# SwiGLU in three 256-column matmuls, and TensorE's tiles on a 256 B grid with the weights 64 B and 192 B off it

## The chip, the cores and the metric

The kernel runs on one core of a Trainium2 chip, in float32 throughout. The metric is the time of one execution on the device, in microseconds (us). The kernel before takes 1268.25 us in the median of three runs (1267.49 to 1269.01).

## What is computed

Two layers over a sequence of 256 positions of width 1024. Per layer: a SwiGLU block, a mixer, a second SwiGLU block. Cut to what matters here:

```python
for l in range(DEPTH):                                   # 2
    x = x + 0.5 * swiglu(rms_norm(x, ffn1_norm[l]), ffn1_w_gate[l], ffn1_w_up[l], ffn1_w_down[l])
    h = rms_norm(x, mix_norm[l])
    proj = h @ w_in[l] + b_in[l]                         # 1024 -> 7176: q k v f xr gr gA gR
    ...                                                  # attention with forget gates; conv + RG-LRU scan
    merged = sigmoid(g_attn) * y_attn + sigmoid(g_rnn) * y_rnn
    x = x + merged @ w_out[l]
    x = x + 0.5 * swiglu(rms_norm(x, ffn2_norm[l]), ffn2_w_gate[l], ffn2_w_up[l], ffn2_w_down[l])
# swiglu(x, g, u, d) = (silu(x @ g) * (x @ u)) @ d, 1024 -> 2816 -> 1024
```

## The kernel before

**Products.** Activations lie transposed (128 channels by 256 positions). For float32 accuracy on TensorE's fast `float32r` format every operand is split into a high part and a low rest: `split` (line 270) copies the high part on ScalarE and subtracts on VectorE. A product of one 128x128 weight block with one 128x256 block of activations is hi*hi + hi*lo + lo*hi, accumulated in a PSUM bank. It comes in two forms (`product`, line 252):

- `mm3` (line 246): three matmuls of 256 columns. The stationary operand is the high weight block in the first two and the low one in the third; each matmul loads its stationary block anew. The mixer's column products take this form: per layer 32 blocks of 8 for xr, gr, gA and gR (256 products), 24 blocks of 8 for the two branch outputs and the merge (192), and 16 in the recurrence (`recurrence`), 464 in all.
- `sides`: one matmul of 512 columns with the high weights, over the high and the low activations side by side (the low half falls into the bank's second half), and one of 256 columns with the low weights. `total` (line 261) then adds the two halves: a copy on ScalarE into the tile `tot` and an addition on VectorE. SwiGLU takes this form (`SIDES = True`): 22 x 2 x 8 products for gate and up and 176 for the way down, 528 a block, 2112 in the four blocks, with 52 calls of `total` a block.

The q, k, v projections (`rows` in `mix`) turn the roles round: activations are stationary and 512 columns of weights stream, 192 threes of 512-column matmuls in both layers.

**Weights.** They arrive in pieces of 1 MB (`wr<-ws` in the trace, three tiles `wr`), are split half a piece at a time (`split_half`, line 364) and wait as a pair of 128x1024 tiles, high and low, either in the eight tiles `W` or in free ones of the 21 tiles `R`. The moving activations are the tile `xs` (the normed input) or tiles `R` (hidden values, branch outputs) or `S`. A planner walks over the steps in order while the program is built; it gives each engine's queue its order, by modelled costs, and splits weights ahead where ScalarE and VectorE have room.

**Where tiles lie.** SBUF tiles are placed one after another in order of first use, each rounded up to 32 B, after a 16 KiB area for DMA descriptors. `R` is 1036 floats wide, so neighbouring ones start 4160 B apart, which is 64 B more than a multiple of 256. In the program that this kernel builds the starts, modulo 256, are: `xs` and all `W` 128; `R0`, `R1`, `R2`, `R3`, `R4`, ... 0, 64, 128, 192, 0, ...; `S` 0, 0, 0, 128, 128. The trace leaves buffer numbers out. In the built program the stretches quoted below use these (starts modulo 256):

| stretch, us | moving | high weights | low weights |
|---|---|---|---|
| 371.8 to 383.8 | xs 128 | W 128 | W 128 |
| 309.5 to 312.0 | xs 128 | R1 64 | R3 192 |
| 406.6 to 408.0 | R17, R1 64 | W3 128 | W2 128 |
| 417.8 to 419.2 | R17, R1 64 | W1 128 | W0 128 |
| 486.1 to 497.4 and 511.3 to 522.4 | xs 128 | W 128 | W 128 |

Blocks inside a tile are a multiple of 512 B apart, so each block of a tile has its tile's start modulo 256.

Of the kernel before, what the change touches and what calls it, by code (L numbers as in the profile page):

```python
# [23 lines left out]
F32 = mybir.dt.float32  # L24
F32R = mybir.dt.float32r
# [23 lines left out]
AHEAD = 20  # L49
SLACK = 2.0  # L50
EARLYX = -0.4
SIDES = True


def f32(ap):
# [138 lines left out]
class Trunk:  # L194
    def __init__(self, ctx, tc, ws, xT, prm, wf, wbd, b_in, out):
        self.tc = tc
        self.ws, self.xT_in, self.prm, self.wf, self.wbd, self.b_in, self.out = ws, xT, prm, wf, wbd, b_in, out
        pool = lambda name, **k: ctx.enter_context(tc.tile_pool(name=name, **k))
        self.const = pool("const", bufs=1)
        self.sb = pool("sb", bufs=1)  # L200
        self.ps = pool("ps", bufs=1, space=bass.MemoryType.PSUM)
        self.dram = pool("dram", bufs=1, space=bass.MemoryType.DRAM)
        ctx.enter_context(tc.manual_schedule())
        nc = tc.nc
        self.clock = c = Clock()
        self.made = {}
        self.PE, self.ACT, self.DVE, self.POOL, self.SP = (Queue(c, nm, e) for nm, e in (
            ("PE", nc.tensor), ("ACT", nc.scalar), ("DVE", nc.vector), ("POOL", nc.gpsimd), ("SP", nc.sync)))
        self.big = Places(c, lambda i, dt: self.t([128, 1036], f"R{i}", 1, dt), 21)
        self.halves = Places(c, lambda i, dt: self.t([128, 1024], f"W{i}", 1, dt), 8)  # L210
        self.small = Places(c, lambda i, dt: self.t([128, 512], f"S{i}", 1, dt), 5)
        self.banks = Places(c, lambda i, dt: self.ps.tile([128, 512], F32, tag=f"B{i}", name=f"B{i}", bufs=1), 8)
        self.steps, self.tasks, self.starts = [], [], []
        self.n_halves = self.s = 0
        self.hl, self.r, self.rb, self.raw, self.acc, self.xs_ok = {}, {}, {}, {}, {}, set()
        self.phase = 0


    def t(self, shape, tag, bufs, dt=F32):
        tl = self.sb.tile(shape, dt, tag=tag, name=tag, bufs=bufs)  # L220
        old = self.made.setdefault(tag, [])
        if len(old) >= bufs:
            self.clock.touch[tl.tensor.name] = self.clock.touch.get(old[-bufs], 0.0)
        old.append(tl.tensor.name)
        return tl
# [3 lines left out]
            self.push()  # L229
        return places.take(dt)  # L230

    def slot(self, shape, dt=F32):

        tl = self.take(self.big, dt)
        return tl, self.view(tl, shape)

    @staticmethod
    def view(tl, shape):
        v = tl[:, :math.prod(shape)]
        if len(shape) == 1:  # L240
            return v
        names = "abcd"[:len(shape)]
        return v.rearrange(f"p ({' '.join(names)}) -> p {' '.join(names)}", **dict(zip(names, shape)))
# [108 lines left out]

    def load_piece(self, p, w=slice(0, 2048)):
        if p not in self.raw:
            self.raw[p] = self.t([128, 2048], "wr", 3)
        self.SP.dma_start(out=self.raw[p][:, w], in_=self.ws[p, :, w])

    def split_places(self):
# [2 lines left out]
            return self.halves  # L361
        return self.big if len(self.big.idle) >= SPARE else None

    def split_half(self, j):
        while self.loaded < self.n_halves // 2 and self.loaded <= j // 2 + 2:
            self.load_piece(self.loaded)
            self.loaded += 1
        places = self.split_places()
        hi, lo = (places.take(F32R)[:, :1024] for _ in range(2))
        raw = self.raw[j // 2][:, (j % 2) * 1024:(j % 2 + 1) * 1024]  # L370
        self.split(hi, lo, raw)
        self.hl[j] = hi, lo, places
        if j % 2:
            del self.raw[j // 2]

    def first_halves(self):

        for j in range(2):
            self.hl[j] = *(self.halves.take(F32R)[:, :1024] for _ in range(2)), self.halves
        for i, (j, c) in enumerate(((0, 0), (1, 0), (0, 1), (1, 1))):  # L380
            for k in (2 * i, 2 * i + 1):
                self.scale_x(0, "ffn1", k)
            w = slice(c * 512, c * 512 + 512)
            self.split(self.hl[j][0][:, w], self.hl[j][1][:, w], self.raw[0][:, j * 1024 + c * 512:j * 1024 + c * 512 + 512])
        del self.raw[0]
# [62 lines left out]
    def new_x(self, phase, l, norm, k):  # L448

        yield self.when(self.x)  # L450
        if k == 0:
            self.xs = self.t([128, 8, 512], "xs", 1, F32R)
        self.scale_x(l, norm, k)
        self.xs_ok.add((phase, k))
        yield self.when(after=0.5)
        self.squares(phase, k)
        if k == 7:
            self.spawn(self.stats(phase), "stats")
# [40 lines left out]
    def setup(self):  # L499
        c = self.const  # L500
        self.cpad = c.tile([128, 128], F32, name="cpad")
        self.DVE.memset(self.cpad, 0.0)
        self.fpad = c.tile([128, 256], F32, name="fpad")
        self.POOL.memset(self.fpad, 0.0)
        self.prm_sb = c.tile([128, L, NP_], F32, name="prm")
        self.ACT.dma_start(out=self.prm_sb, in_=self.prm)
        self.ACT.activation(self.t([128, 1], "ss", 4), self.cpad[:, 0:1], AF.Silu)
        self.x = c.tile([128, 8, 256], F32, name="x")
        q = lambda i: slice(512 * i, 512 * i + 512)
        for i, w in enumerate((0, 2, 1, 3)):  # L510
            self.SP.dma_start(out=self.x[:, 2 * i:2 * i + 2], in_=self.xT_in[:, 2 * i:2 * i + 2])
            self.load_piece(0, q(w))
        self.load_piece(1, slice(0, 1024))
        self.load_piece(1, slice(1024, 2048))
        self.load_piece(2)
        warm = self.take(self.banks)
        for _ in range(WARM):
            self.PE.matmul(warm[:, 0:128], self.cpad, self.cpad, start=True, stop=True)
        self.banks.give(warm)
        self.ident = c.tile([128, 128], F32, name="ident")  # L520
        self.POOL.memset(self.ident, 1.0)
        self.POOL.affine_select(out=self.ident, in_=self.ident, compare_op=ALU.is_equal, fill=0.0, base=0,
                                pattern=[[-1, 128]], channel_multiplier=1)
        self.ones = c.tile([128, 128], F32, name="ones")
        self.POOL.memset(self.ones, 1.0)
        self.mhalf = c.tile([128, 8], F32, name="mhalf")
        self.DVE.memset(self.mhalf, -0.5)
        self.xs = self.t([128, 8, 512], "xs", 1, F32R)
        self.xs_ok |= {(0, k) for k in range(8)}
        self.spawn(self.first_stats(), "stats")  # L530
        self.starts.append((30, self.constants, "bias"))
# [59 lines left out]
    def ffn(self, l, name):  # L591
# [3 lines left out]

        def gu_steps(f):
            js = self.half(), self.half()
            banks = {}

            def step(i, ks):  # L600
                def fn(wh, wl):
                    if ks[0] == 0:

                        self.need(lambda: phase in self.rb or len(self.banks.idle) > 1, "stats", "x")
                        banks[i] = self.take(self.banks)
                    for k in ks:
                        w = slice(k * 128, k * 128 + 128)
                        self.product(banks[i], wh[:, w], wl[:, w], self.x_rhs(phase, k), k == 0, k == 7, SIDES)
                return Step(js[i], fn, [(self.glu(f, phase, banks, st), "glu")] if i and ks[-1] == 7 else [])
            if f == 0 and not self.steps:  # L610
                order = [(i, ks) for ks in (range(4), range(4, 8)) for i in range(2)]
            elif f == 0:
                order = [(0, range(4)), (0, range(4, 7)), (1, range(4)), (1, range(4, 7)), (0, range(7, 8)), (1, range(7, 8))]
            else:
                order = [(i, ks) for i in range(2) for ks in (range(4), range(4, 8))]
            self.steps += [step(i, ks) for i, ks in order]

        for f in range(NF):
            gu_steps(f)
        halves = [self.half() for _ in range(NF)]  # L620
        runs = {}
        for i in range(8 * NF):
            d, f = divmod(i, NF)
# [49 lines left out]
    def mix(self, l):  # L673
# [6 lines left out]
        def rows(i):  # L680

            nm, n = PROJ[i]
            js = [self.half() for _ in range(4)]
            banks = {}

            def step(h, t):
# [88 lines left out]
    def block_diagonal(self, M):  # L775
        for n in range(2):
# [1 line left out]
            raw, w = self.slot([4, 2, 128])  # L778
            self.SP.dma_start(out=w, in_=self.wbd[M["l"], n])
            yield self.when(raw, must=lambda: len(self.big.idle) >= 4)  # L780
            hi, lo = (self.slot([4, 2, 128], F32R) for _ in range(2))
            self.split(hi[1], lo[1], w)
            self.big.give(raw)
            M["wd", n] = hi, lo
# [419 lines left out]
```

## Time and profile before

| | us |
|---|---|
| median of three runs | 1268.25 |
| the profiled execution: its own time | 1267.97 |
| its span, first to last instruction | 1266.3 |
| TensorE busy, matmuls | 1255.5 |
| VectorE busy | 937.3 |
| ScalarE busy | 755.0 |

What lies around the span is 1.67 us; the median run is 0.28 us above the profiled one. Matmuls are pipelined and overlap in the records (a 256-column matmul is shown some 280 ns long, though the next begins 113 to 120 ns after it), so a matmul's cost is read as the distance from its start to the start of the next: the time from one row's start to the next row's start, over the count of the row.

### The profile page before, as it was taken

What the parts mean: (1) busy time and instruction counts of PE and PEld (TensorE: products, weight loads), DVE (VectorE), ACT (ScalarE), POOL (GpSimd) and SP (SyncE); (2) the same over time, 40 slices, a digit from 0 to 9 for tenths busy, and PEclk for the clock granted to TensorE, in tenths of its full rate; (3) what the DMA queues carried; (4) which work ended last, traced back from release to release, by engine and by line L of the source; (5) the groups of instructions that cost most, each with busy time, mean ns of one, the idle gap of its engine ahead of it and who ended that gap; (6) DMA issues with size and microseconds to landing.
All of it is one profiled execution on the core that took longest, in us unless ns stands there. A gap on an engine that the chain in (4) does not pass through costs nothing.

```text
span 1266.3 us, 20160 instructions
## 1 busy us (share of the span) xinstructions
PE 1255.5 (99%) x7928; PEld 1130.3 (89%) x7928; DVE 937.3 (74%) x1613; ACT 755.0 (60%) x1406; POOL 35.7 (3%) x48
## 2 busy tenths in 40 slices
PE   8999999999999999999999999999999999999998
PEld 7888888889999998888888888878999999888887
DVE  6777867668759977776677776775786798777763
ACT  6555646675795665555555554565658856555541
POOL 1000001120000000000000000011100000000000
PEclk9999999999999999999999999999999999999999
DMA  8355666533445755444555554563344466544451
GB/s 286 138 181 197 233 217 241 207 111 124 157 143 207 278 182 196 171 166 167 200 199 202 174 190 167 208 236 133 141 151 166 167 237 232 196 172 161 168 186 46
DMA packets 36015, 232.21 MB, mean 183 GB/s; under 512 B 4528, under 2 KB 5712, under 8 KB 9040
## 3 DMA queue, kind: packets, MB, share of 16 engines
q1 hardware_dynamic: 35776, 230.79, 51.2%
q8 instruction: 62, 1.02, 0.3%
q14 instruction: 33, 0.27, 0.1%
q10 hardware_dynamic: 144, 0.13, 0.0%
HBM read 229.84 MB, written 1.06 MB: 182 GB/s over the span
## 4 chain that ended last, share of the span: by engine, by line
PE 95%; DMA 2%; DVE 1%; ACT 1%; issue 1%; SPq 0%; POOL 0%; DVEq 0%; ACTq 0%
PE B L151 95%; DMA wr<-ws 1%; DVE W L151 1%; ACT W L151 0%; DMA R<-cd 0%; DMA prm<-prm 0%; DVE lg L151 0%; DVE S L151 0%; SPq L151 0%; DVE acc L151 0%; DVE nm L151 0%; DVE tot L151 0%; DVE sq L151 0%; POOL rst L151 0%; ACT dp L151 0%
## 5 line engine op out<-in xcount | busy, mean ns | idle before, releaser
L151 PE MATMUL B<-xs,W 128*128 128x256 f32 (+1 forms) x2992 | 463.9, 314 | 4.2 <-DVE xs L151 2.5
L151 DVE TENSOR_TENSOR W<-wr,W 128x1024 fp32r<-128x1024 f32 (+1 forms) x281 | 340.2, 1214 | 165.7 <-ACT W L151 163.0
L151 PEld LDWEIGHTS B<-xs,W 128*128 128x128 f32 x2992 | 416.2, 190 | 43.3 <-ACT W L151 2.6
L151 ACT CAST W<-wr 128x1024 fp32r<-128x1024 f32 (+1 forms) x281 | 290.3, 1041 | 154.2 <-PE B L151 129.8
L151 PE MATMUL B<-R,W 128*128 128x256 f32 (+1 forms) x1840 | 281.4, 312 | 0.1
L151 PEld LDWEIGHTS B<-R,W 128*128 128x128 f32 x1840 | 254.3, 188 | 22.6 <-DVE R L151 0.4
L151 PE MATMUL B<-xs,R 128*128 128x512 f32 (+1 forms) x1360 | 236.1, 330 | 0.0
L151 PEld LDWEIGHTS B<-xs,R 128*128 128x128 f32 x1360 | 202.7, 188 | 25.5
L151 DVE TENSOR_TENSOR R<-wr,R 128x1024 fp32r<-128x1024 f32 x145 | 175.1, 1220 | 32.7 <-ACT R L151 32.3
L151 ACT CAST R<-wr 128x1024 fp32r<-128x1024 f32 x145 | 148.7, 1043 | 1.1 <-DMA wr<-ws 1.0
L151 ACT ACTIVATE S<-S 128x256 f32<-128x256 f32 x88 | 36.8, 418 | 169.4 <-DVE S L151 169.4
L151 PE MATMUL B<-R,R 128*128 128x256 f32 (+2 forms) x784 | 124.1, 312 | 0.0
L151 PEld LDWEIGHTS B<-R,R 128*128 128x128 f32 x784 | 108.1, 188 | 8.9
L151 DVE TENSOR_TENSOR tot<-B,tot 128x256 f32<-128x256 f32 x208 | 86.9, 418 | 35.9 <-ACT tot L151 35.9
L151 ACT COPY tot<-B 128x256 f32<-128x256 f32 x208 | 75.7, 367 | 50.1 <-PE B L151 48.3
L151 PE MATMUL B<-R,xs 128*128 128x512 f32 x312 | 79.7, 401 | 0.0
L151 PEld LDWEIGHTS B<-R,xs 128*128 128x128 f32 x312 | 57.1, 188 | 11.9
L151 PE MATMUL B<-W,xs 128*128 128x512 f32 x264 | 66.4, 397 | 0.0
L151 DVE TENSOR_TENSOR R<-S,R 128x256 fp32r<-128x256 f32 x88 | 36.8, 422 | 37.5 <-ACT R L151 37.5
L151 PEld LDWEIGHTS B<-W,xs 128*128 128x128 f32 x264 | 48.8, 188 | 10.3
L151 POOL TENSOR_TENSOR rst<-rst,mhalf 128x4 f32<-128x4 f32 (+1 forms) x22 | 27.4, 1247 | 966.1 <-DVE rst L151 959.0
L151 DVE TENSOR_TENSOR S<-tot,S 128x256 f32<-128x256 f32 x88 | 37.4, 425 | 3.0
(117 smaller groups left out, 726.4 us busy)
## 6 DMA issues: line engine op xcount, KB each, us to landing
wr<-ws SPq DMA_DIRECT2D x210, 1024.0 KB, 4.9
bias<-b_in SPq DMA_DIRECT2D x8, 256.0 KB, 4.8
R<-cd SPq DMA_DIRECT2D x4, 512.0 KB, 4.7
R<-wbd SPq DMA_DIRECT2D x4, 512.0 KB, 5.7
x<-xT SPq DMA_DIRECT2D x4, 256.0 KB, 5.8
wr<-ws SPq DMA_DIRECT2D x4, 256.0 KB, 6.2
wr<-ws SPq DMA_DIRECT2D x2, 512.0 KB, 7.8
out<-x SPq DMA_DIRECT2D x8, 128.0 KB, 1.7
```

The costliest lines, as they stand in the source:

```text
L151: return fn(*args, **kw)
```

## The change

- `SIDES` is off: SwiGLU's products take the three-matmul form too, and `total` returns the bank's first half without the copy and the addition.
- Tiles that TensorE reads (`wr`, `xs`, `W`, `R`, `S`) move to a pool of their own, `ops`, placed first. `R` and `W` are 1088 floats (4352 B = 17 x 256), so all these tiles start at the same place modulo 256. The descriptor area shrinks from 16 to 4 KiB, which makes room.
- Weights don't fill their tile from its start: `AT = 16, 48`, in floats, puts the high part 64 B and the low part 192 B into the tile. The block diagonal weights of the recurrence do the same. The q, k, v weights, which are the moving operand, stay at 0 (`spots`). Moving activations start at 0 of their tile.

```diff
-SIDES = True
+SIDES = False
+
+AT = 16, 48
+FFN_AT = AT
...
+        self.ops = pool("ops", bufs=1)
...
-        self.big = Places(c, lambda i, dt: self.t([128, 1036], f"R{i}", 1, dt), 21)
-        self.halves = Places(c, lambda i, dt: self.t([128, 1024], f"W{i}", 1, dt), 8)
-        self.small = Places(c, lambda i, dt: self.t([128, 512], f"S{i}", 1, dt), 5)
+        self.big = Places(c, lambda i, dt: self.t([128, 1088], f"R{i}", 1, dt, self.ops), 21)
+        self.halves = Places(c, lambda i, dt: self.t([128, 1088], f"W{i}", 1, dt, self.ops), 8)
+        self.small = Places(c, lambda i, dt: self.t([128, 512], f"S{i}", 1, dt, self.ops), 5)
...
-    def slot(self, shape, dt=F32):
+    def slot(self, shape, dt=F32, at=0):
         tl = self.take(self.big, dt)
-        return tl, self.view(tl, shape)
+        return tl, self.view(tl, shape, at)
...
+    def where(self, j):
+        return self.spots.get(j, AT)
...
-        hi, lo = (places.take(F32R)[:, :1024] for _ in range(2))
+        hi, lo = (places.take(F32R)[:, at:at + 1024] for at in self.where(j))
...
+            self.spots.update(dict.fromkeys(js, FFN_AT))      # gate, up; the same for down
...
+            self.spots.update(dict.fromkeys(js, (0, 0)))      # q, k, v rows
...
-            hi, lo = (self.slot([4, 2, 128], F32R) for _ in range(2))
+            hi, lo = (self.slot([4, 2, 128], F32R, at) for at in AT)
...
-    nc = bacc.Bacc("TRN2", target_bir_lowering=False, num_devices=1)
+    nc = bacc.Bacc("TRN2", target_bir_lowering=False, num_devices=1, dynamic_dma_scratch_size=4096)
```

## Rows read from the trace of the kernel before

**Rows 1.** The page: span, busy time and share of each engine, TensorE's clock by slices.
```profile
span 1266.3 us, 20160 instructions
...
PE 1255.5 (99%) x7928; PEld 1130.3 (89%) x7928; DVE 937.3 (74%) x1613; ACT 755.0 (60%) x1406; POOL 35.7 (3%) x48
...
PEclk9999999999999999999999999999999999999999
```

**Rows 2.** Whom TensorE waited for: us in total, times, longest.
```profile
PE B L151 <- DVE xs L151: 2.5, 1, 2.5
PE B L151 <- DVE mhalf L151: 1.1, 1, 1.1
PE B L151 <- DVE W L151: 0.8, 1, 0.8
```

**Rows 3.** Busy time by stretch, instruction counts in brackets; columns in its first line.
```profile
core 0: us, PE busy (x) PEld busy (x) DVE busy (x) ACT busy (x) POOL busy (x), PEclk, DMA share, GB/s
7.30:35.00 27.70, 26.00 (x135) 21.48 (x136) 21.90 (x33) 18.44 (x30) 2.26 (x3) 0.94 0.87 321
35.00:198.60 163.60, 163.51 (x928) 141.95 (x928) 125.46 (x210) 93.60 (x169) 0.00 (x0) 1.00 0.53 190
280.00:383.80 103.80, 103.80 (x862) 103.38 (x861) 75.81 (x140) 77.69 (x145) 1.79 (x4) 1.00 0.42 148
383.80:451.70 67.90, 67.90 (x579) 67.90 (x578) 64.96 (x98) 41.77 (x59) 0.00 (x0) 1.00 0.66 233
451.70:637.20 185.50, 185.50 (x1065) 162.63 (x1063) 134.53 (x216) 101.73 (x177) 1.60 (x1) 1.00 0.51 180
637.20:822.90 185.70, 185.70 (x1064) 162.51 (x1063) 136.83 (x220) 103.09 (x180) 1.61 (x1) 1.00 0.53 190
903.80:1007.90 104.10, 104.10 (x861) 103.67 (x860) 76.54 (x142) 76.80 (x140) 1.72 (x4) 1.00 0.42 148
1007.90:1075.90 68.00, 68.00 (x578) 68.00 (x577) 64.12 (x98) 41.26 (x58) 0.00 (x0) 1.00 0.63 232
1075.90:1261.70 185.80, 185.77 (x1064) 162.36 (x1062) 122.44 (x196) 89.23 (x156) 1.60 (x1) 1.00 0.45 158
```

**Rows 4.** TensorE's timeline, three-matmul products in the mixer: start, us, operands, count.
```profile
371.82 12.16 PE L151 MATMUL B<-xs,W 128*128 128x256 f32 x100
383.82 11.36 PE L151 MATMUL B<-R,W 128*128 128x256 f32 x94
```

**Rows 5.** TensorE's timeline from 309.7 to 312.4 us.
```profile
309.49 2.66 PE L151 MATMUL B<-xs,R 128*128 128x256 f32 x22
311.98 0.64 PE L151 MATMUL B<-xs,W 128*128 128x256 f32 x4
```

**Rows 6.** TensorE's timeline, two stretches of 11 matmuls between equal addresses.
```profile
406.78 1.41 PE L151 MATMUL B<-R,W 128*128 128x256 f32 x11
...
417.92 1.46 PE L151 MATMUL B<-R,W 128*128 128x256 f32 x11
```

**Rows 7.** TensorE's timeline in SwiGLU; each row holds 512- and 256-column matmuls in turn.
```profile
486.06 11.46 PE L151 MATMUL B<-xs,W 128*128 128x512 f32 x64
497.36 14.14 PE L151 MATMUL B<-xs,R 128*128 128x512 f32 x80
511.34 11.26 PE L151 MATMUL B<-xs,W 128*128 128x512 f32 x64
522.44 0.39 PE L151 MATMUL B<-xs,R 128*128 128x512 f32 x1
```

**Rows 8.** Mean length of a 256-column matmul's record, and `total`'s two instructions, by line.
```profile
L151 PE MATMUL B<-R,W 128*128 128x256 f32 x1328 | 242.3, 281 | 0.0
...
L151 DVE TENSOR_TENSOR tot<-B,tot 128x256 f32<-128x256 f32 x208 | 86.9, 418 | 35.9 <-ACT tot L151 35.9
L151 ACT COPY tot<-B 128x256 f32<-128x256 f32 x208 | 75.7, 367 | 50.1 <-PE B L151 48.3
```

**Rows 9.** The end of the chain that ended last: start, us, what.
```profile
1261.71 0.38 ACT tot L151
1262.09 0.02 issue
1262.11 0.44 DVE tot L151
```

More of the change, by code (lines that the diff above doesn't have):

```diff
@@ L214, in __init__, with t @@
         self.n_halves = self.s = 0
+        self.spots = {}
         self.hl, self.r, self.rb, self.raw, self.acc, self.xs_ok = {}, {}, {}, {}, {}, set()
         self.phase = 0
-    def t(self, shape, tag, bufs, dt=F32):
-        tl = self.sb.tile(shape, dt, tag=tag, name=tag, bufs=bufs)
+    def t(self, shape, tag, bufs, dt=F32, pool=None):
+        tl = (pool or self.sb).tile(shape, dt, tag=tag, name=tag, bufs=bufs)
         old = self.made.setdefault(tag, [])
@@ L230, in take, with view @@
         return places.take(dt)
-    def slot(self, shape, dt=F32):
+    def slot(self, shape, dt=F32, at=0):
         tl = self.take(self.big, dt)
-        return tl, self.view(tl, shape)
+        return tl, self.view(tl, shape, at)
     @staticmethod
-    def view(tl, shape):
-        v = tl[:, :math.prod(shape)]
+    def view(tl, shape, at=0):
+        v = tl[:, at:at + math.prod(shape)]
         if len(shape) == 1:
@@ L354, in load_piece @@
         if p not in self.raw:
-            self.raw[p] = self.t([128, 2048], "wr", 3)
+            self.raw[p] = self.t([128, 2048], "wr", 3, F32, self.ops)
         self.SP.dma_start(out=self.raw[p][:, w], in_=self.ws[p, :, w])
@@ L378, in first_halves @@
         for j in range(2):
-            self.hl[j] = *(self.halves.take(F32R)[:, :1024] for _ in range(2)), self.halves
+            self.hl[j] = *(self.halves.take(F32R)[:, at:at + 1024] for at in self.where(j)), self.halves
         for i, (j, c) in enumerate(((0, 0), (1, 0), (0, 1), (1, 1))):
@@ L451, in new_x @@
         if k == 0:
-            self.xs = self.t([128, 8, 512], "xs", 1, F32R)
+            self.xs = self.t([128, 8, 512], "xs", 1, F32R, self.ops)
         self.scale_x(l, norm, k)
@@ L527, in setup @@
         self.DVE.memset(self.mhalf, -0.5)
-        self.xs = self.t([128, 8, 512], "xs", 1, F32R)
+        self.xs = self.t([128, 8, 512], "xs", 1, F32R, self.ops)
         self.xs_ok |= {(0, k) for k in range(8)}
@@ L620, in ffn @@
         halves = [self.half() for _ in range(NF)]
+        self.spots.update(dict.fromkeys(halves, FFN_AT))
         runs = {}
```

## The prediction

> **What bounds the kernel now.** I began with the page: TensorE is busy 99% of the span, at the full granted clock in every slice, while VectorE is at 74% and ScalarE at 60% [rows 1]. Then the waits: all that TensorE waited for is a few us, nearly all in the opening [rows 2]. So the end moves only with the rate at which TensorE starts matmuls, and the question is what sets the distance from one start to the next. The stretches give it by stage [rows 3]: SwiGLU after the opening takes 163.6 + 185.5 + 185.7 + 185.8 = 720.6 us. These hold 464 + 3 x 528 = 2048 products (928 matmuls, two to a product, in the first; 528 a block after). The counts of the last three are 8 or 9 over 1056; for these small matmuls of the norm I allow 0.6 us a block, so one product takes (720.6 - 1.8) / 2048 = 351 ns. In the mixer the two stretches of branch outputs and merge have 192 three-matmul products in 67.9 and 68.0 us, 354 ns each.
>
> Next, the timeline, start to start. Where `xs` streams against weights in `W`, all starting 128 B past a multiple of 256, 100 matmuls take 383.82 - 371.82 = 12.00 us: 120 ns each, 360 a product [rows 4]. Where the same `xs` streams against weights in `R1` and `R3`, 64 B behind and 64 B ahead of it modulo 256, 22 matmuls take 311.98 - 309.49 = 2.49 us: 113.2 each, 340 a product [rows 5]. Same form, same clock, same moving tile; only the weights' addresses differ. [...]
>
> That isn't the whole of it. Two stretches with hidden values 64 B behind `W` run at different rates [rows 6]: with one record's 281 ns [rows 8] taken off the length, 10 intervals take 1.13 and 1.18 us, so 113 and 118 ns, 340 and 354 a product, at addresses equal modulo 256. A stream at a good offset can keep a tight rhythm or a loose one. SwiGLU's two-matmul form shows two rhythms as well: 32 products of `xs` with `W` take 11.30 us from 486.06 and 11.10 from 511.34, 353 and 347 each; the 40 with `R` between take 349.5 [rows 7].
>
> **The change, part by part.** My unit is the product in tight rhythm, 340 ns, and f is the share of products in the loose one, 353.5 (3 x 117.8, rows 6). All is set against the profiled execution, 1266.3 us of span.
>
> - SwiGLU takes one matmul and one weight load more per product, but no more columns (3 x 256 for 512 + 256). Its high weights lie 64 B, its low ones 192 B past the moving operand: the two distances of rows 5, exchanged. That exact order has no long stretch in this trace, which is the weakest place of the sum. 2048 x 340 ns = 696.3, with the 1.8 us of norms 698.1 against 720.6: -22.5 us. At 353.5 it is +5.1. The opening, 7.3 to 35 us, has the DMA engines 87% busy at 321 GB/s and the clock and waits of a start [rows 3]; its 64 products wait for weights, and I give it no gain (if half of it came, 0.4 us more).
> - The mixer's three-matmul products get the same offsets. In the branch stages 2 x 192 x (353.8 - 340) = 5.3 us. In the column stages (103.8 and 104.1 us, rows 3) 2 x 256 products go from 360 [rows 4] or, where weights lie in `R`, a little less; I take 358, so 512 x 18 = 9.2 us. The 32 products of the recurrence run at a few ns over 340 to 360 and I leave them out (0 to 0.6 us). Sum -14.5; in loose rhythm throughout, -0.1 and -2.3.
> - The q, k, v rows stay at offset 0 modulo 256, as those weights that lie in `W` now are; those in `R` lose their assorted offsets. No row decides between them, so I put 0, with 192 x 3 matmuls x 4 ns = 2.3 us either way (4 ns is half the spread of rows 4 and 5, rounded up). The attention's small float32 matmuls move likewise: 0, within 0.5 us.
> - `total` loses 208 copies and 208 additions, 75.7 us of ScalarE and 86.9 of VectorE [rows 8]. TensorE hides all of them but those of the last output block, where copy and addition stand in the chain after the last matmul, 0.38 + 0.44 + 0.02 [rows 9]: -0.85 us. With the rest gone the planner splits weights earlier, which nothing on the path asks for.
> - A faster TensorE needs its weights sooner. VectorE is at 95.7% in the branch stage, 64.96 of 67.90 us [rows 3]; at 340 that stage is 65.3 us. It still fits, and part of what VectorE does there is splitting for the SwiGLU after it, where VectorE has room (136.8 of 185.7, less the additions). DMA at 180 to 230 GB/s is far under the 321 of the opening. I put 0; if VectorE did bind there it would cost at most what the stage gains, 2 x 2.6 us.
> - The smaller descriptor area costs nothing that a row shows: loads are issued by SP's queue. The other layout is a matter of place only.
>
> Sum at f = 0: -22.5 - 14.5 - 0.85 = -37.9, a span of 1228.4. Each tenth of f costs a tenth of 2944 products (2048 + 384 + 512) x 13.5 ns, so 4 us. After each break (a head's matmuls, a change of operand) a stream needs a product or two to settle, so f = 0 isn't to be had; I take f = 0.1. Span 1232.4; with 1.67 around it 1234.1, and 0.28 for the median run: **1234 us**.
>
> [...]
>
> **The rivals.**
> 1. *The loose rhythm wins part of the time.* Uniform offsets mean that a stream which falls into 118 ns has nothing to throw it out until the next break. For it: rows 6, at equal addresses. Against: rows 5, steady to its end with weights on both sides. f from 0.25 to 0.9 gives 1240 to 1266.
> 2. *It wins everywhere* (f near 1): SwiGLU +5.1, mixer -2.4, end -0.85: +2, 1270 us, no change that shows. It is the point from which the change stops paying.
> 3. *Slower: the third matmul costs what it costs where it now stands.* If rows 5 owe their pace to something else than the offset (the moving tile, the moment), SwiGLU's third matmul brings with it the 120 ns of rows 4: 2048 x (360 - 351) = +18.4 us, the mixer gains nothing, 1286 us. It decides from 351 ns a product on. For it: the mixer's long stretches, all at 354 to 360. Against: rows 4 and 5 differ in the offset alone. [...] A half of it, 355 ns, gives +8 and 1276.
> 4. *The change doesn't do what it says*, the offsets end up elsewhere: all tiles are multiples of 256 B, so the distance between any two is what the code says. I give it nothing of its own.
>
> **How the numbers follow.** Forecast (f under 0.25, 1228 to 1240): 0.54. Rival 1: 0.27. Rival 2, within 0.2% of 1268.25 (about what a measurement can tell from no change): 0.08. Rival 3: 0.11. Faster by over 0.2%: 0.54 + 0.27 = 0.81; same 0.08; slower 0.11. The range leaves out 2 in 10: rivals 2 and 3 make 0.19, so it reaches from 1227 (f = 0, with the small terms on the good side) to 1264, the far end of rival 1.
>
> **What the profile after would show.** SwiGLU's rows of 256-column matmuls at 113.3 ns from start to start (right), 118 (rival 1 or 2) or 120 (rival 3); the three full SwiGLU blocks at about 181 us instead of 185.5 to 185.8; the branch stages at 65 to 66; no tile `tot`, VectorE near 850 us; TensorE's waits still a few us. If waits for `W` from VectorE grow in the branch stages, its cover was misjudged. If the blocks come out under 180, the floor of 340 was wrong.

## The result, and the profile after

The changed kernel takes 1245.4 us in the median (1244.9 to 1245.9) beside 1268.4 for the kernel before: a ratio of 0.982, with a 95% interval of 0.980 to 0.984. It is faster by 23 us where 34 were forecast. 1245.4 lies in the middle of the range of 1227 to 1264, but outside the 1228 to 1240 that were held most likely.

The page of the changed kernel's profiled execution (1245.86 us), its span, TensorE's busy time and clock, and the shares of the chain that ended last by engine; to be read beside [rows 1]:

```profile
span 1244.1 us, 24052 instructions
...
PE 1226.0 (99%) x10040; PEld 1194.2 (96%) x10040; DVE 851.8 (68%) x1411; ACT 697.5 (56%) x1192; POOL 36.0 (3%) x48
...
PEclk9999999999999999999999999999999899999999
...
PE 88%; DVE 6%; ACT 2%; DMA 2%; issue 1%; SPq 0%; ACTq 0%; DVEq 0%
```

TensorE still looks 99% busy, but two things are new: one slice of its clock is an 8, and 8% of the chain that ended last lies on VectorE and ScalarE, where the page of the kernel before has 2%. The waits say the same. Here are TensorE's in the changed kernel (us in total, times, longest), 14.1 us where [rows 2] add up to 4.4, and most of them on ScalarE's and VectorE's copies of weights (`W`) and on `R`:

```profile
PE B L154 <- ACT W L154: 4.5, 3, 3.0
PE B L154 <- DVE R L154: 3.9, 2, 2.4
PE B L154 <- DVE W L154: 1.8, 5, 0.6
PE B L154 <- DVE sq L154: 1.7, 3, 1.0
PE B L154 <- ACT rb L154: 1.1, 1, 1.1
PE B L154 <- DVE mhalf L154: 1.1, 1, 1.1
```

The stretches of the changed kernel, columns as in [rows 3]: first SwiGLU block after the opening, then q, k, v rows, columns and branch outputs of layer 1, two SwiGLU blocks, the same three of layer 2, the last SwiGLU block:

```profile
35.00:193.80 158.80, 158.80 (x1398) 158.80 (x1398) 103.62 (x155) 79.26 (x115) 0.00 (x0) 1.00 0.55 193
193.80:274.70 80.90, 79.94 (x397) 66.43 (x397) 58.12 (x141) 53.49 (x144) 12.32 (x13) 1.00 0.53 188
274.70:374.40 99.70, 99.69 (x861) 99.03 (x861) 74.70 (x140) 75.54 (x140) 1.73 (x4) 1.00 0.44 153
374.40:442.30 67.90, 66.02 (x579) 65.62 (x579) 65.64 (x100) 41.73 (x60) 0.00 (x0) 1.00 0.66 235
442.30:622.70 180.40, 180.40 (x1592) 180.35 (x1591) 112.04 (x165) 88.21 (x126) 1.60 (x1) 1.00 0.53 184
622.70:803.20 180.50, 180.50 (x1592) 180.45 (x1592) 115.11 (x169) 88.88 (x128) 0.70 (x1) 1.00 0.57 196
803.20:883.50 80.30, 80.05 (x398) 66.40 (x397) 55.61 (x122) 53.87 (x143) 12.44 (x13) 1.00 0.55 192
883.50:990.00 106.50, 102.92 (x861) 101.96 (x860) 76.04 (x141) 76.34 (x141) 1.78 (x4) 0.97 0.42 144
990.00:1059.60 69.60, 67.19 (x578) 66.99 (x577) 65.66 (x98) 40.96 (x58) 0.00 (x0) 0.98 0.64 225
1059.60:1240.30 180.70, 180.68 (x1592) 180.43 (x1591) 100.30 (x146) 76.04 (x106) 1.60 (x1) 1.00 0.47 163
```

Set against [rows 3], and against 280 - 198.6 and 903.8 - 822.9 for the rows of q, k, v, which lie between its stretches:

| | before, us | after, us | moved | forecast at 340 ns |
|---|---|---|---|---|
| SwiGLU after the opening | 720.6 | 700.4 | -20.2 | -22.5 |
| q, k, v rows, both layers | 162.3 | 161.2 | -1.1 | 0 |
| columns, layer 1 | 103.8 | 99.7 | -4.1 | -4.6 |
| columns, layer 2 | 104.1 | 106.5 | +2.4 | -4.6 |
| branch outputs, layer 1 | 67.9 | 67.9 | 0 | -2.6 |
| branch outputs, layer 2 | 68.0 | 69.6 | +1.6 | -2.7 |
| from the last matmul to the end of the span | 4.6 | 3.8 | -0.8 | -0.85 |

The sum is -22.2, the difference of the spans. SwiGLU gave nearly all that was forecast, the mixer next to nothing. Where it went stands in the difference between a stretch's length and TensorE's busy time: 0.96, 0.01, 1.88, 0.25, 3.58 and 2.41 us in the six stretches of the mixer, 9.1 in all (before, 0.9, all of it in the q, k, v rows). The granted clock of 0.97 and 0.98 in two of them is the rest.

The rate itself is the good one. TensorE's timeline of the changed kernel (start, length, operands, count) in the second SwiGLU block, and in the second layer's columns around the longest wait:

```profile
489.47 13.76 PE L154 MATMUL B<-xs,R 128*128 128x256 f32 x120
503.07 11.04 PE L154 MATMUL B<-xs,W 128*128 128x256 f32 x96
...
950.21 24.80 PE L154 MATMUL B<-xs,W 128*128 128x256 f32 x216
...
978.00 0.67 PE L154 MATMUL B<-xs,W 128*128 128x256 f32 x2 [2.99 <-ACT W L154]
979.26 10.93 PE L154 MATMUL B<-xs,W 128*128 128x256 f32 x70 [0.59 <-DVE W L154]
990.03 2.20 PE L154 MATMUL B<-R,W 128*128 128x256 f32 x18
```

503.07 - 489.47 is 13.60 us for 120 matmuls, 113.3 ns each and 340 a product. The mixer's 216 from 950.21, with one record's 0.28 us taken off, run at 24.52 / 215 = 114.0. Then TensorE stands still for 2.99 us and, after two matmuls, for 0.59, and the next 70 take 990.03 - 979.26 = 10.77 us, 2.8 more than at 113.3. The granted clock tells why, in the stretches of the same kernel behind the wait (columns as above):

```profile
979.20:981.20 2.00, 1.94 (x9) 1.94 (x10) 2.00 (x5) 1.22 (x3) 0.00 (x0) 0.50 0.56 66
981.20:985.00 3.80, 3.80 (x20) 3.80 (x20) 2.92 (x4) 3.77 (x6) 0.00 (x0) 0.50 1.00 375
985.00:990.00 5.00, 5.00 (x45) 5.00 (x45) 1.73 (x3) 5.00 (x11) 0.00 (x0) 1.00 0.50 146
```

It is at 0.50 until 985 and at 1.00 after that. This wait of 3 us so cost nearly 3 us more behind it. The wait of 2.4 us at 1012 in the branch outputs was followed by 5.6 us that were partly at the lower level (0.71 from 1014.4 to 1017.5, 0.67 to 1020); the wait of 1.5 us at 425 by none (1.00 from 425.2 to 430).

What TensorE waited for at 975 was ScalarE's queue. Its timeline in the changed kernel, the number in brackets being the idle time before a row:

```profile
967.66 1.04 ACT L154 CAST W<-wr 128x1024 fp32r<-128x1024 f32 x1
971.50 1.28 ACT L154 ACT_TABLE_LOAD   x1 [2.80 <-DVE R L154]
972.80 2.01 ACT L154 ACTIVATE R<-R 128x1024 f32<-128x1024 f32 x2
974.81 1.28 ACT L154 ACT_TABLE_LOAD   x1
976.11 0.91 ACT L154 ACTIVATE R<-R,hb 128x256 f32<-128x256 f32 x2
976.92 2.92 ACT L154 CAST W<-wr 128x1024 fp32r<-128x1024 f32 x3
```

A step of the recurrence (the two activations of 1024 columns from 972.80) waits 2.80 us for VectorE and brings two table loads of 1.28 us; the split of the weights that TensorE needs stands behind all this and begins at 976.92. ScalarE is busy 76.34 us of the 106.5. It isn't short of time; the order in its queue holds the weights up.

### The profile page after: what moved, and what is told of

It is laid out like the page before. It is cut to its first block, busy times and chain, and to the rows that moved or that the text cites. A ratio compares the mean times of both kernels' runs of the same rounds, so it can differ in the third digit from the quotient of the medians.

```text
span 1244.1 us, 24052 instructions
## 1 busy us (share of the span) xinstructions
PE 1226.0 (99%) x10040; PEld 1194.2 (96%) x10040; DVE 851.8 (68%) x1411; ACT 697.5 (56%) x1192; POOL 36.0 (3%) x48
## 4 chain that ended last, share of the span: by engine, by line
PE 88%; DVE 6%; ACT 2%; DMA 2%; issue 1%; SPq 0%; ACTq 0%; DVEq 0%
PE B L154 88%; DVE R L154 3%; DVE W L154 2%; DMA wr<-ws 2%; ACT R L154 1%; ACT W L154 1%; DMA prm<-prm 0%; ACT L154 0%; SPq L154 0%; DVE acc L154 0%; DVE sq L154 0%; DVE x L154 0%; ACT sq L154 0%; ACT rb L154 0%; ACTq L154 0%
## 5 line engine op out<-in xcount | busy, mean ns | idle before, releaser
L154 DVE TENSOR_TENSOR W<-wr,W 128x1024 fp32r<-128x1024 f32 (+1 forms) x263 | 319.4, 1215 | 221.9 <-ACT W L154 220.4
L154 PE MATMUL B<-xs,W 128*128 128x256 f32 x3480 | 416.6, 279 | 7.1 <-ACT W L154 4.5
L154 PE MATMUL B<-R,W 128*128 128x256 f32 x2304 | 268.3, 277 | 4.3 <-DVE R L154 3.9
L154 PE MATMUL B<-xs,R 128*128 128x256 f32 x2280 | 269.0, 277 | 0.0
L154 PEld LDWEIGHTS B<-xs,R 128*128 128x128 f32 x2280 | 263.2, 188 | 0.2
L154 DVE TENSOR_TENSOR R<-wr,R 128x1024 fp32r<-128x1024 f32 x163 | 197.6, 1220 | 66.2 <-ACT R L154 65.8
L154 PE MATMUL B<-R,R 128*128 128x256 f32 (+1 forms) x1024 | 125.9, 279 | 0.0
L154 ACT CAST R<-S 128x256 fp32r<-128x256 f32 x88 | 34.9, 402 | 38.6 <-DVE S L154 38.6
L154 DVE TENSOR_TENSOR S<-B,S 128x256 f32<-128x256 f32 x88 | 36.4, 418 | 17.1 <-PE B L154 15.0
L154 ACT ACTIVATE xs<-x,prm 128x256 fp32r<-128x256 f32 x48 | 23.9, 506 | 23.9 <-DVE x L154 21.4
```

What stands on the lines that cost most here:

```text
L154: return fn(*args, **kw)
```

## The experiments

Two theories were set against each other in most of them. On the rate: the starts of the operands decide it, or something else does. On the mixer: the order of the work in the queues of VectorE and ScalarE kept back its gain, or these engines have no more room.

**SwiGLU's weights back at 0.** The form and the mixer as in the changed kernel.

```diff
-FFN_AT = AT
+FFN_AT = 0, 0
```

> The changed kernel with one thing undone: SwiGLU's weights start at 0 of their tiles, so modulo 256 B they start where the moving operand does; the three-matmul form stays, the mixer keeps 64 B and 192 B. Theory A (the offset between weights and moving operand sets the pace): SwiGLU's 256-column matmuls go from 113.3 to 120 ns from start to start, a full SwiGLU block from 180.5 to 528 x 360 ns + 0.6 = 191 us, the kernel from 1245.4 to about 1245 + 41 = 1286 us. Theory B (what brought the pace is the common 256 B grid of all tiles, or the form, whatever the offset): blocks stay at 180 to 181 us and the kernel within 2 us of 1245.

Measured: 1284.9 us, ratio 1.013 (1.011 to 1.014). TensorE's timeline of this kernel in the second SwiGLU block:

```profile
499.81 14.56 PE L154 MATMUL B<-xs,R 128*128 128x256 f32 x120
514.22 6.04 PE L154 MATMUL B<-xs,W 128*128 128x256 f32 x49
```

14.41 us for 120 matmuls, 120.1 ns each where the changed kernel has 113.3. The same products in the same form, with the weights 64 and 192 B elsewhere in their tiles: 39 us. The first theory's 1286 us held. Three matmuls without the offsets lose against the two-matmul form (1261.1 us with the weights at the same starts, below), and the third rival's 1286 us was close to the price of that, though its sum had no gain in the mixer, which keeps its offsets here. So the starts of the operands alone change the pace, 120.1 against 113.3 ns, though no trace here shows in which part of the chip that arises.

**The mixer's weights back at 0**, SwiGLU's at 64 and 192 B.

```diff
-AT = 16, 48
-FFN_AT = AT
+AT = 0, 0
+FFN_AT = 16, 48
```

> The changed kernel with SwiGLU's offsets kept and the mixer's weights back at 0 of their tiles. The mixer's column and branch stages took 99.7 + 67.9 and 106.5 + 69.6 us in the changed kernel, with 14 us of TensorE's waits and of half clock among them, although its matmuls came at 113.3 ns. Theory A (TensorE outruns VectorE and ScalarE there): at 120 ns a matmul the waits go, and the stages take about what they took before, 104 + 69 us in each layer, so the kernel comes out at 1245.4 + 2.5 = 1248 us, nearly as fast as with the offsets. Theory B (the waits have nothing to do with TensorE's pace): the slower matmuls are added to them, 928 x 20 ns = 18.6 us, and the kernel takes 1264 us.

Measured: 1254.5 us, ratio 0.989 (0.988 to 0.990), between the two theories. Its mixer products run at 120 ns a matmul again (columns of 104.4 us in layer 1), and in layer 2 TensorE still waits 1.7 us for `W` from ScalarE and 2.8 for `R` from VectorE. The mixer's offsets are worth 9 us net in the changed kernel; as these waits are there without the mixer's faster rate, they don't come from that alone.

**The two-matmul form in the new layout**, SwiGLU's weights at 0, the mixer's at 64 and 192 B.

```diff
-SIDES = False
+SIDES = True
...
-FFN_AT = AT
+FFN_AT = 0, 0
```

> The old two-matmul form in SwiGLU with its weights at 0 of their tiles, on the new layout; the mixer keeps its offsets of 64 B and 192 B. It tells the layout and the mixer's offsets apart from SwiGLU's new form. Theory A (SwiGLU's gain comes of the form with the offsets; the mixer's of nothing that lasts): SwiGLU blocks at 347 to 353 ns a product, 183.5 to 187 us, and the mixer at 100 to 107 and 66 to 70 us; the kernel 1258 to 1268 us. Theory B (the 256 B grid alone speeds both up): blocks at 181 us and the kernel at 1245.

Measured: 1261.1 us, ratio 0.995 (0.993 to 0.996). Here the mixer's six stretches sum to 495.7 us against 506.1 before, 10.4 of the 14.5 that were forecast for it: the columns give 3.4 and 4.4, the branch outputs 0.4 and 0.2. In both stretches of branch outputs VectorE is busy 65.4 of 67.5 and 65.6 of 67.8 us, and TensorE waits 1.6 and 1.8. With this order of work VectorE sets the pace of that stage. The time is inside the first theory's range, but the mixer's gain does last, against what that theory said.

One kernel was not tried: the two-matmul form with SwiGLU's weights at 64 and 192 B. So it is open how much of SwiGLU's gain the form adds to the offsets. In the kernel before, some two-matmul products lie at these distances by chance (the addresses of the built program set beside its trace): ten stretches of 4 to 8 products, 349 to 353 ns a product in the mean of each, no faster than the 347 and 353 at equal starts [rows 7]. They are too short to settle it.

**The planner's price of a matmul.** The planner takes a 256-column matmul to last 116.9 ns; it lasts 113.3 now. The same line also prices one of 512 columns, which the q, k, v rows use; it goes from 226.7 to 220.0 ns with the edit.

```diff
-            return 2 * max(2 * n / 2400 + 0.003, 0.06) if two else max(n / 2330 + 0.007, 0.108)
+            return 2 * max(2 * n / 2400 + 0.003, 0.06) if two else max(n / 2400 + 0.0067, 0.108)
```

> The changed kernel with one number of the planner corrected: a 256-column matmul is modelled at 113.4 ns, as measured, in place of 116.9. Nothing else changes but the order and the placement of work that follows from it. Theory A (the planner takes TensorE to be slower than it now is, and queues splits and other work of ScalarE and VectorE too late): the waits of the mixer, some 10 us with the half clock behind them, shrink to under 4 us, and the kernel takes 1233 to 1238 us. Theory B (VectorE at 97% of the branch stage and the fixed chain of the recurrence bind, whatever the order): the waits stay, 1242 to 1247 us.

Measured: 1242.3 us, ratio 0.980 (0.978 to 0.981), inside what the second theory gives. But the profile doesn't bear that theory out: layer 2 now has 99.3 us for its columns (890.19 to 989.45) and 66.8 for its branch outputs (to 1056.20), and what is lost sits in one place of layer 1. The first rows of these stages and of the SwiGLU block behind them, then TensorE's longest wait and, behind it, ScalarE's, in this kernel:

```profile
890.19 2.90 PE L154 MATMUL B<-xs,W 128*128 128x256 f32 x24
...
989.45 5.72 PE L154 MATMUL B<-R,W 128*128 128x256 f32 x49
...
1056.20 2.72 PE L154 MATMUL B<-xs,R 128*128 128x256 f32 x21
```

```profile
PE B L154 <- ACT R L154: 8.1, 1, 8.1
```

```profile
399.94 1.14 ACT L154 CAST R<-R 128x512 fp32r<-128x512 f32 x2 [7.73 <-DVE R L154]
```

One branch output of the recurrence came 8 us late. VectorE was busy all that while, with splits of weights and readings of PSUM among the recurrence's own steps. An engine without room would be late in both layers. So the order was tried next.

**The planner's order.** The measured price, and three constants: background work may be queued on VectorE and ScalarE while they are booked up to 7 us ahead of TensorE (3.5 before), and weights are split up to 28 steps ahead (20), but only where both engines are booked at most 0.5 us ahead (2.0).

```diff
-ROOM = 3.5
+ROOM = 7.0
...
-AHEAD = 20
-SLACK = 2.0
+AHEAD = 28
+SLACK = 0.5
```

> The changed kernel, with the planner's price of a 256-column matmul set to the measured 113.3 ns (as in the run with that price alone) and three of its constants changed: it may queue background work on VectorE and ScalarE when they are booked up to 7 us ahead of TensorE (3.5 before), it splits weights up to 28 steps ahead (20) but only where both engines are booked at most 0.5 us ahead (2.0). The computation and the offsets are the same. Theory A: what held the mixer back is only the order in which the planner queues work on VectorE and ScalarE; the engines have the room. Then the one wait of 8.1 us that the measured price alone left in the first layer's branch stage shrinks to under 2, the half clock after it goes with it, and the time is 1227 to 1235. Theory B: VectorE or ScalarE is the bound of the mixer once its products take 340 ns, whatever the order; then the waits move to other places and the sum stays, 1240 to 1246.

Measured: 1229.2 us (1228.4 to 1229.8), ratio 0.969 (0.968 to 0.971), the fastest of all. TensorE's waits in this kernel, its four stretches of columns and branch outputs, and its second SwiGLU block (436.8 to 617.3):

```profile
PE B L154 <- ACT W L154: 2.3, 3, 1.8
PE B L154 <- DVE W L154: 1.5, 2, 0.8
PE B L154 <- DVE mhalf L154: 1.1, 1, 1.1
```

```profile
269.80:371.50 101.70, 100.71 (x867) 99.84 (x866) 85.09 (x155) 76.34 (x141) 1.81 (x4) 1.00 0.45 163
371.50:436.80 65.30, 65.30 (x578) 65.30 (x577) 55.56 (x86) 36.97 (x54) 0.00 (x0) 1.00 0.58 215
436.80:617.30 180.50, 180.50 (x1593) 180.45 (x1592) 115.82 (x167) 89.95 (x128) 0.70 (x1) 1.00 0.55 192
...
876.70:978.40 101.70, 100.71 (x867) 99.83 (x866) 85.10 (x155) 76.32 (x141) 1.82 (x4) 1.00 0.46 163
978.40:1043.70 65.30, 65.30 (x579) 65.30 (x577) 55.54 (x86) 36.98 (x54) 0.00 (x0) 1.00 0.60 214
```

The branch outputs take 65.3 us, 340 a product, without a wait: VectorE does 55.6 us there where it did 65.6, and the 10 us stand in the stretch before (85.1 for 74.7). The rows of q, k, v take 79.0 us in either layer. A layer of the mixer takes 79.0 + 101.7 + 65.3 = 246.0 us where it took 253.1 and 253.0: 14.1 us for the two. SwiGLU's blocks are those of the changed kernel. VectorE and ScalarE had the room; the order in which the planner gave them their work kept back the mixer's gain.

**Which part of the order counts.** The 7 us alone with the measured price; then all three constants with the old price.

```diff
-ROOM = 3.5
+ROOM = 7.0
```

> As the run before, with the measured price and the 7 us alone; the two constants of splitting ahead as in the changed kernel. Theory A: the late queueing of background work (the recurrence's chain) is what counts, and splitting ahead little; 1230 to 1238, the 8.1 us wait gone. Theory B: 1240 to 1246.

> The changed kernel with the planner's three constants (7 us, 28 steps, 0.5 us) but its old price of 116.9 ns. If the order alone counts and the price only shifts it, 1232 to 1242; if the planner must have the right price of a matmul, because it thinks that TensorE is later than it is and queues work late, its waits stay as in the changed kernel, 1242 to 1248.

Measured: 1239.0 us, ratio 0.977 (0.976 to 0.979), for the first; 1235.0, ratio 0.974 (0.972 to 0.975), for the second. In the first the 8.1 us wait is gone, as expected, but TensorE waits 4.4 us for `W` from ScalarE, 1.9 of them in the opening and 2.5 in the columns; the time fell between the ranges of the two theories, so splitting ahead counts as well. In the second the order does most of the work with the wrong price: 10.4 of the 16.2 us that lie between the changed kernel and the fastest. The right price alone gives 3.1, and the two together 2.7 more than the sum of either alone.

**The same order in the kernel before.** Layout and forms of product as before, with the price and the three constants above.

> The kernel before, its layout and forms of product unchanged, with the same price and the same three constants. TensorE there waits for 6 us in all, nearly all of it in the opening, so the order has nothing to give: 1263 to 1270. If the order were worth as much without the offsets, 1255 or less; then the gain of the first run of this call would not belong to the change.

Measured: 1277.1 us, ratio 1.007 (1.006 to 1.009). It is slower than either answer had it: TensorE's listed waits grow from 4.4 to 11.1 us. So this order at this price gives the kernel before nothing. The price of 113.3 ns is not that kernel's own (113 to 120 ns in [rows 4, 5, 6]), and the three constants at the old price were not tried on it. But its listed waits are 4.4 us in all [rows 2], so no order could have taken 39 us off it while its matmuls kept their rate.

**Other distances between the operands.** High and low weights both 128 B into their tiles; both 64 B; the changed kernel's two exchanged.

```diff
-AT = 16, 48
+AT = 32, 32
```

> The changed kernel with high and low weights both 128 B into their tiles, in SwiGLU and in the mixer, in place of 64 B and 192 B. Theory A (a distance of an odd multiple of 64 B between weights and moving operand is what counts): at 128 B the 256-column matmuls come at 118 to 120 ns, as in the kernel before at distances of 0 and 128, SwiGLU blocks take 187 to 191 us, and the kernel 1270 to 1290 us. Theory C (any distance but 0 will do): blocks stay at 180.5 us and the kernel at 1245.

```diff
-AT = 16, 48
+AT = 16, 16
```

> The changed kernel with high and low weights both 64 B into their tiles, so that every weight load stands at the same distance from the moving operand. If only the odd multiple of 64 B counts, 113.3 ns throughout, blocks of 180.5 us, 1245 us. If the two rhythms that the kernel before showed at this distance (113 and 118 ns at equal addresses) are a matter of high and low weights standing alike, the loose one comes back: between 118 ns throughout, blocks of 187 us and 1268 us, and 113.3 in a part of the stretches.

```diff
-AT = 16, 48
+AT = 48, 16
```

> The changed kernel with the two offsets exchanged: high weights 192 B, low ones 64 B into their tiles, the order that the stretch from 309.5 us of the kernel before had. Theory A: the order makes no difference, 113.3 ns from start to start, blocks of 180.5 us, 1245 us within 3. If the order counts, the loose rhythm of 118 ns appears and the kernel takes up to 1268 us.

Measured: both at 128 B 1283.9 us, ratio 1.013 (1.010 to 1.016); both at 64 B 1252 us, from two executions 8 us apart, ratio 0.988 (0.980 to 0.995); exchanged 1277.7 us (1271.9 to 1283.2), ratio 1.007 (1.004 to 1.010). The first theory's answers held for both at 128 B, where a row of 120 matmuls runs at (14.40 - 0.28) / 119 = 118.7 ns:

```profile
502.76 14.40 PE L154 MATMUL B<-xs,R 128*128 128x256 f32 x120
```

The kernel with both at 64 B shows two rhythms in one execution, here in its second SwiGLU block, its second layer's columns and its last SwiGLU block:

```profile
489.46 13.76 PE L154 MATMUL B<-xs,R 128*128 128x256 f32 x120
...
911.92 20.03 PE L154 MATMUL B<-xs,W 128*128 128x256 f32 x168
...
1109.31 5.82 PE L154 MATMUL B<-xs,W 128*128 128x256 f32 x48
1114.96 11.47 PE L154 MATMUL B<-xs,R 128*128 128x256 f32 x96
```

(13.76 - 0.28) / 119 is 113.3 ns, (20.03 - 0.28) / 167 is 118.3, (1114.96 - 1109.31) / 48 is 117.7. In the three SwiGLU blocks before the second layer's mixer it keeps the tight rhythm: 72 matmuls of that layer's columns start at 902.53 us, 0.32 us after the same ones of the changed kernel (902.21). In that layer's columns it has the loose one for the 168 matmuls from 911.92, with no wait of TensorE in front of them, and the tight one again for the 216 from 951.55. Behind a wait of 3.01 us it is tight again once the clock is back (193 matmuls from 990.18); behind the next wait, 2.99 us from 1012 to 1015, it is loose to the end.

The exchanged pair shows both rhythms as well, here in its first and second SwiGLU block and, later, in the second layer's columns:

```profile
134.23 8.32 PE L154 MATMUL B<-R,W 128*128 128x256 f32 x72
...
490.79 14.43 PE L154 MATMUL B<-xs,R 128*128 128x256 f32 x120
...
968.33 24.78 PE L154 MATMUL B<-xs,W 128*128 128x256 f32 x216
```

With 0.28 us taken off each, these are 113.2, 118.9 and 114.0 ns. It has 340 ns a product in its first block and, nearly throughout, in the first layer's columns: 24 matmuls of the second block start at 482.23 us, only 0.92 us after the same ones of the changed kernel (481.31). In the second block it has 357, and it falls behind the changed kernel by 18.12 us up to the 216 matmuls (968.33 for 950.21) and by 28.5 up to the end of the span (1272.6 for 1244.1). At 1277.7 us it takes longer than the 1268 that the second answer allowed.

**The exchange without the waits.** The fastest kernel with the offsets exchanged: does a stream lose the tight rhythm by waiting?

```diff
-AT = 16, 48
+AT = 48, 16
```

> The kernel with the measured price and the three constants, with the two offsets exchanged: high weights 192 B, low weights 64 B into their tiles, everything else the same. With the old order of work that exchange gave products of 340 ns in the first SwiGLU block and of 353 to 360 from the second on. Theory A: a stream keeps its rhythm until it has to wait, and the waits of the mixer threw it into the loose one. With hardly a wait left, it stays at 340 and the time is 1229 to 1236. Theory B: the order of the offsets itself can't hold the tight rhythm; then the three later SwiGLU blocks run at 353 to 360 again, 1584 products by 13 to 20 ns, 21 to 32 us, with a little in the mixer: 1250 to 1265.

Measured: 1272.9 us, ratio 1.003 (1.002 to 1.005); more than the second theory's range, since the loose rhythm is there from the first block on (it ends at 197.5 us, 190.8 in the fastest kernel), and in the first layer's mixer too (columns 103.6 us for 101.7, branch outputs 68.5 for 65.3). The second SwiGLU block and the first layer's branch outputs of this kernel:

```profile
380.10:448.60 68.50, 68.50 (x578) 68.50 (x577) 55.71 (x86) 36.99 (x54) 0.00 (x0) 1.00 0.57 205
448.60:637.80 189.20, 189.20 (x1592) 189.15 (x1591) 115.88 (x167) 89.86 (x128) 0.70 (x1) 1.00 0.52 183
```

No idle time in either, and 189.2 us against 180.5, 68.5 against 65.3; with the 0.6 us allowed for the norm, 188.6 / 528 and 68.5 / 192 are 357 ns a product. So this pair falls into the loose rhythm without a wait. Nor does the order of the distances force it: with the old order of work the same pair had 113.2 ns a matmul in its first block. What is shown is that 64 and 192 B kept the tight rhythm, but for a few products behind a wait or a break (in the changed kernel eight matmuls from 896.84 us at 118 to 124 ns, behind three small ones), in the changed kernel and in the stretches read of the one with the measured price alone (113.3 ns for the 96 matmuls from 419.56) and of the fastest (SwiGLU blocks of 180.4 to 180.6 us, branch outputs of 65.3), and that 192 and 64 B did so in neither of theirs. What makes a stream change its rhythm stays open.

## Why the prediction was right or wrong

**The rate, right.** The step that rests on [rows 4, 5] held: with the start of the operands alone changed, a matmul takes 113.3 or 120.1 ns. The third rival (a third matmul at 120 ns, 1286 us) is close to what comes without SwiGLU's offsets, 1284.9. The three full SwiGLU blocks take 180.4, 180.5 and 180.7 us where about 181 was given.

**f, on the wrong side.** A tenth of the products was put into the loose rhythm, 4 us. In SwiGLU there are next to none: (180.4 + 180.5 + 180.7 - 1.8) / 1584 = 340.8 ns. The 340.8 includes what is lost at the ends of the blocks. By the time alone, 1245.4 us falls to the first rival, to whose loose rhythm the forecast gave 1240 to 1266 us (the range stopped at 1264). But that rival's mechanism is not there; waits and a lower clock in the mixer took the time that it would have taken. The range was made wide for another reason than the one that it was needed for, so that it held the result was luck.

**The order of the two distances, a step that was called weak and was.** [rows 5] have the high weights 64 B behind the moving operand (192 modulo 256) and the low ones 64 ahead. The forecast took the change's order to be the same thing. It isn't: the order of [rows 5], used throughout, gives 340 ns a product in some stretches and 357 over whole blocks, so a stretch of 22 matmuls doesn't tell what a stream settles to. Both orders have odd multiples of 64 B between weights and moving operand, so an odd multiple alone does not set the pace. The change had the better order; from these rows that couldn't be known. It was luck in that step.

**The end, right.** -0.8 for -0.85, no tile `tot`, and VectorE at 851.8 us for 850.

**The mixer, wrong in size: -1.2 us for -14.5.** The rate was there; what failed is the step "a faster TensorE needs its weights sooner", put at 0 and bounded by 2 x 2.6 us. Two mistakes are in it. First, it weighed sums: VectorE's 64.96 us against a stage of 65.3. That only says that the work fits if its order is right, and the planner makes the order for matmuls of 116.9 ns, slower than they now are, with constants that were chosen before the change. In the branch outputs VectorE set the pace (65.6 us of work, no gain in layer 1), which was the danger named, with about the price named there (2.6 us against the forecast; 4.3 in layer 2, where the slower clock adds to it). In the second layer's columns, not named at all, ScalarE's queue held up the weights behind a step of the recurrence: 3.6 us of waiting where 4.6 of gain were booked. The forecast says nothing of ScalarE there, which was idle a quarter of that stage [rows 3]. Second, the bound left out what a wait does to the clock: behind the waits of 2.99 and 2.4 us TensorE ran at a granted clock of 0.50, and of 0.71 and 0.67, for some 6 us. For the first that cost 2.8 us more, and the second is the reason that layer 2's branch outputs, at a clock of 0.98, ended 1.6 us slower than before.

The balance: -37.9 at 340 ns, +13.3 in the mixer, +2.3 in SwiGLU are, but for rounding, the -22.2 measured. Put in the other order, with the measured price, the queues give the sum back: 1228.1 us of span in the fastest kernel where the sum at f = 0 was 1228.4. Its parts agree less well, so that the sum comes this close is in part luck. The mixer gives 14.1 us for 14.5: the branch outputs 5.3, as booked, but the rows of q, k, v 4.3 where nothing was booked and the columns 4.5 where 9.2 were. Part of this is where the one stage ends and the next begins, since some small matmuls of the attention heads fall into the columns there. SwiGLU and the opening give 23.3 for 22.5. Between 7.3 and 35 us, in the opening, this kernel has 216 matmuls where the changed kernel has 192, for which nothing had been booked.

**The signs that were named.** "Waits still a few us" was wrong, 14.1. "Branch stages at 65 to 66" was wrong for the changed kernel (67.9 and 69.6) and right once the order fits (65.3). "If waits for `W` from VectorE grow, its cover was misjudged" pointed the right way, though the waits were mostly for `W` from ScalarE and `R` from VectorE.

## What to carry to other kernels

When the bounding engine gets faster by some per cent, look at the order of work in every queue that feeds it, also those of engines that are idle a quarter of the time: what counts is what stands ahead of the piece that is due next, and an order that was made for the old rate can put it too late. After such a change give the planner its measured duration and try its order again; here that was worth 16 us on top of the 23. And where TensorE streams matmuls back to back, compare the distance from start to start at several starts of the operands, over whole blocks rather than a few dozen matmuls.

## What the runs showed of the hardware

- The starts of moving operand and weights, modulo 256 B, change the pace of 256-column `float32r` matmuls (mean granted clock 0.993 to 0.999 in these runs). With the moving operand at 0:

| high, low weights at, B | ns from start to start | kernel |
|---|---|---|
| 64, 192 | 113.3 | changed kernel |
| 64, 64 | 113.3 in three blocks, 117.7 in the last and 118.3 in part of the second layer's columns | both at 64 B |
| 192, 64 | 113.2 in the first block, 118.9 in the second, 114.0 in part of the second layer's columns; in the other order of work 118.9 in the second block | exchanged |
| 128, 128 | 118.7 | both at 128 B |
| 0, 0 | 120.1 | SwiGLU's weights at 0 |

- All starts tried are multiples of 64 B. Of the pairs, 64 and 192 B alone kept the tight rhythm of 113.3 ns wherever it was read, in the changed kernel, in the one with the measured price alone and in the fastest, but for a few products behind a wait or a break.
- Why the order of the two counts, and what puts a stream into the one rhythm or the other, no trace shows: it lists when matmuls and weight loads begin and end, not their reads of SBUF. It stays open.
- A wait of about 3 us on TensorE cost up to nearly as much again: behind the 2.99 us of the changed kernel the granted clock was 0.50 for some 6 us, and the 70 matmuls there took 2.8 us more. In the kernel with both at 64 B the same 70 took 9.57 us behind a wait of 3.01, 1.6 more. Behind a wait of 1.50 us the clock stayed at 1.00.
